# The opening blocks of a fused transformer layer: six single contraction tiles in place of two singles and two pairs

## The chip, the cores and the metric

One core of a Trainium2 chip runs the whole layer in one launch. The metric is the device time of one execution in microseconds (us). The kernel before was run three times: 2598.96, 2601.55 and 2601.9 us, median 2601.55.

## The reference

The layer has 256 latent tokens `x` and 256 context tokens `ctx`, each of width D = 2048, and condition vectors `c` and `c_ctx`. It runs a half-step feed-forward network (FFN), a token mixer (attention and a bidirectional mLSTM), and a second FFN, in float32. Only its beginning matters here:

```python
mod_l = (silu(c) @ w_mod + b_mod).reshape(B, 9, D)       # latent tokens; mod_c likewise from c_ctx
def adaln(x, g, mod, i):
    return rms_norm(x, g) * (1 + mod[:, i + 1, None, :]) + mod[:, i, None, :]
def half_step_ffn(x, mod, i, g, w_up, w_down):
    h = adaln(x, g, mod, i)
    a, b = split(h @ w_up, 2)
    return x + 0.5 * mod[:, i + 2, None, :] * ((silu(a) * b) @ w_down)
```

Before the first product `h @ w_up` can start, the shift (`mod[0]`) and the scale (`mod[1]`) are needed: two matrix products of the condition vectors with 2048 x 2048 slices of `w_mod`, 16 MB each. They belong to the channels of `h`, and the contraction of `h @ w_up` runs over just these channels.

## The kernel before

The 2048 channels are 16 contraction tiles of 128. The opening stage (lines 462 to 690) works through them in blocks, listed in `BLOCKS` (line 45): tiles 0 and 1 are blocks of their own, the other 14 go in pairs. For each block (k0, k1) the loop at line 648 does four things.

- *Modulation sums* (`mod_sums`, line 564). The weights `w_m0` come in 32 loads of 1 MB (`mod_unit`, line 557) into four buffers called `mraw`. TensorE multiplies them with the condition vectors, held as the stationary operand `cP` of 32 columns; the result goes through ScalarE (`row`), is turned by TensorE (`mod_turned`, line 588), and VectorE adds it up into `SH` (shift) and `SC` (scale). A single block takes one load for its shift and one for its scale. A pair takes four: the shift of its first tile comes in another layout and is summed by VectorE (line 660, the "still" sum, one scan for the context and one for the latent tokens, with the conditions spread over all partitions in `cB`), the shift of its second tile goes through TensorE, and so does the scale of both, in two loads with matmuls twice as wide.
- *Turning and scaling x.* TensorE turns the block's channels of the normalised tokens (`x_turned`, `to_hT`). ScalarE and VectorE apply scale and shift and split the result into a high and a low part, `hhi` and `hlo` (`x_scaled` and `affine_split`, lines 549 and 380).
- *Products* (`products`, line 407). Six result banks of 128 x 512, the first three pairs of columns of `h @ w_up`, are held in PSUM for the whole stage. Each block adds its tiles to each bank: three matmuls per tile and bank, because float32 is made of high and low parts. The weights of a block are one load (`w_pre`, 384 KB for a single block, 768 KB for a pair) that ScalarE and VectorE split (`split`, line 120) when the generator is stepped a second time. One bank's matmuls are a *unit*; a block has six.
- *Interleaving.* A block's products run while the next block's sums are made: `prods` is the previous block's generator, `following` this block's, and `steps` moves them on.

In a pair, one unit goes behind each of the three groups of modulation sums, one behind the row transposes, and two behind the transposes of x; in a single block two units go behind each of the two groups. TensorE and VectorE keep the written order throughout the stage (`Pinned`), and ScalarE does until the first pair is through (line 686). The first pair also has its products' split (`steps(following)`) and a unit behind the computation of the scale, and later blocks ahead of it. All loads of the stage are issued on SyncE's queue in the written order; the load of a block's products goes ahead of the block's last modulation load. After the stage come the long matmul phases of the first FFN.

Of the kernel before, what the change touches and what calls it, by code (L numbers as in the profile page):

```python
# [41 lines left out]

BLOCKS2 = tuple((k, k + 4) for k in range(0, 16, 4))

BLOCKS = ((0, 1), (1, 2)) + tuple((k, k + 2) for k in range(2, 16, 2))
FB = 4
CB = 512
NCB = D // CB
# [10 lines left out]
def tile_layer(ctx: ExitStack, tc: tile.TileContext, I: dict, out: bass.AP):  # L59
# [16 lines left out]
    def tbank():  # L76
        return ps["tr"].tile([P, 512], F32, tag="tr", name="tr")
# [138 lines left out]
    def scale_of(n, s, kk):  # L216

        vector[0].scalar_tensor_tensor(SC[:, n, s, kk], SC[:, n, s, kk], 1.0, gnT[:, n, kk], op0=ALU.add, op1=ALU.mult)
# [48 lines left out]
    class Beside:  # L267
# [49 lines left out]
        def steps(self):  # L317
            half = None
            while self.n < len(self.items) or self.due or self.late:
                while self.n < len(self.items):  # L320
                    h = self.items[self.n][2]
                    if h != half:
                        half = h
                        conditions({LAT: self.cB}, h, h + 1, (LAT,))
                        self.waits += WAIT
                    if self.n not in self.slots or self.done < np.interp(self.n, *zip((0, 0), *self.pace)) + self.waits:
                        break
                    self.one()
                yield
                self.done += 1  # L330
                for x in [x for x in self.due if x[0] <= self.done]:
                    self.due.remove(x)
                    self.finish(*x[1:])
                if self.late and self.late[0][0] <= self.done:
                    mod_rows_out(*self.late.pop(0)[1:])
# [71 lines left out]
    def products(n_ffn, pre, k0, k1, hhi, hlo, early=False, both=False, middle=False):  # L407

        n = (k1 - k0) * P
        most = min(2 * NPRE, 2048 // n // 2 * 2)

        def load(u0):
            nu = min(most, 2 * NPRE - u0)
            raw = raw_tile(n * nu)

            o = (2 * NPRE * k0 * P + u0 * n) * P  # L420
            tc.keep_in_program_order(nc.sync.dma_start(raw, I[f"w_pre{n_ffn}"][o : o + n * nu * P].rearrange("(p c) -> p c", p=P)))
            return raw, nu

        ahead = [load(0)]
        if early:
            wt = split(ahead[0][0], n * ahead[0][1])
        if both:
            ahead.append(load(most))
        yield
        if middle:  # L430
            wt = split(ahead[0][0], n * ahead[0][1])
            early = True
            yield
        for u0 in range(0, 2 * NPRE, most):
            raw, nu = ahead.pop(0)
            if u0 or not early:
                wt = split(raw, n * nu)
            if u0 + most < 2 * NPRE and not ahead:
                ahead.append(load(u0 + most))
            for u in range(nu):  # L440
                b = pre[(u0 + u) // 2][u % 2]
                ws = [(k, wt(slice(u * n + (k - k0) * P, u * n + (k - k0 + 1) * P))) for k in range(k0, k1)]

                for k, (wh, wl) in ws:
                    tensor[0].matmul(b, wh, hhi[:, k, :], start=k == 0, stop=False)  # L445
                    tensor[0].matmul(b, wl, hhi[:, k, :], start=False, stop=False)  # L446
                for k, (wh, wl) in ws:
                    tensor[0].matmul(b, wh, hlo[:, k, :], start=False, stop=k == KT - 1)
                yield
# [12 lines left out]
    with pool(name="st", bufs=1) as st:  # L462
# [70 lines left out]
        def others(n, act=False):  # L533
            for _ in range(n):
                x, r = rest.pop(0)
                if act:
                    scalar[0].activation(x, x, AF.Copy, scale=r)
                else:
                    vector[0].tensor_scalar(x, x, r, None, op0=ALU.mult)
# [4 lines left out]
        def x_turned(k, s, t, tb=first_tb):  # L544

            o = s * 256 + t * P
            tensor[0].transpose(tb[:, o : o + P], xs0[s, t][:, k * P : (k + 1) * P], ident)
# [9 lines left out]
        def mod_unit():  # L557
            if ready:
                return ready.pop(0)
            raw = st.tile([P, 2048], F32, tag="mraw", name="mraw", bufs=4)  # L560
            tc.keep_in_program_order(nc.sync.dma_start(raw, I["w_m0"][next(unit)]))
            return raw

        def mod_sums(i, k0, k1, last=iter(())):

            n = (k1 - k0) * P
            nk = 2048 // n
            b = tbank()[:, :n]
            for g in range(KT // nk):
                if g == KT // nk - 1:  # L570
                    steps(last)
                raw = mod_unit()
                for j in range(nk):
                    k = nk * g + j
                    q = 32 * (j % 4)
                    tensor[0].matmul(
                        b[q : q + 32, :], cP[:, k, :], raw[:, j * n : (j + 1) * n], start=k < 4, stop=k >= KT - 4, tile_position=(0, q), skip_group_check=True
                    )
                yield
            row = st.tile([P, 256], F32, tag="row", name="row", bufs=3)[:, :n]  # L580
            scalar[0].activation(row, b, AF.Copy)
            turns.append((i, k0, k1, row))

        def biased(i, k0, k1):
            dst = (SH, SC)[i][:, 0, :, k0:k1]
            vector[0].tensor_tensor(dst, dst, bmT[:, i, k0:k1].unsqueeze(1).to_broadcast([P, 2, k1 - k0]), op=ALU.add)

        def mod_turned():
            for i, k0, k1, row in turns:
                p2 = tbank()[:, : (k1 - k0) * P]  # L590
                for j in range(k1 - k0):
                    tensor[0].transpose(p2[:, j * P : (j + 1) * P], row[:, j * P : (j + 1) * P], ident)
                vector[0].tensor_reduce(
                    (SH, SC)[i][:, 0, :, k0:k1], p2.rearrange("p (k j x) -> p x k j", j=4, x=32)[:, 0:2], axis=AX.X, op=ALU.add
                )
                biased(i, k0, k1)
            turns.clear()
# [49 lines left out]
        others(2)  # L647
        for k0, k1 in BLOCKS[1:]:
            kk = slice(k0, k1)
            following = products(1, pre, k0, k1, hhi, hlo, middle=True)  # L650
            if k1 - k0 == 2:
                raw = mod_unit()
            for i in range(2):
                for _ in mod_sums(i, k0 if i else k1 - 1, k1, following if i else iter(())):
                    steps(prods, 3 - (k1 - k0))
                if rest:
                    others(2, True)
                if not i and k1 - k0 == 2:
                    for s in (CTX, LAT):
                        vector[0].scalar_tensor_tensor(  # L660
                            junk.bitcast(FP8), raw, 1.0, cB[:, s, :], op0=ALU.mult, op1=ALU.mult, accum_out=SH[:, 0, s, k0 : k0 + 1], saturate=False
                        )
                    biased(0, k0, k0 + 1)

            if k0 != 2:
                steps(following)
            mod_turned()
            if k0 != 2:
                steps(prods)
            for s in (CTX, LAT):  # L670
                scale_of(0, s, kk)
            if k0 == 2:
                steps(following)
                steps(prods)
            if k1 - k0 == 1:
                tb = tbank()
                for s in (CTX, LAT):
                    for t in range(2):
                        x_turned(k0, s, t, tb)
                x_scaled(k0, tb)  # L680
            else:
                for s in (CTX, LAT):
                    drain(to_hT([xs0[s, 0], xs0[s, 1]], 0, s, hhi, hlo, 256 * s, range(k0, k1)))
            drain(prods)
            prods = following
            if k0 == 2:
                scalar[0] = nc.scalar
            if k1 == KT:
                nc.sync.dma_start(ccd.rearrange("s (k p) -> (s k) p", p=P), cc)
# [1658 lines left out]
def _laid_out(a):  # L2348
# [27 lines left out]

    m["w_m0"] = asc(np.concatenate([u for b in BLOCKS for u in block(*b)]))
    m["w_mt"] = asc(wm[:, 2:].reshape(D, 7, KT, P).transpose(1, 2, 3, 0))
    for n in "12":
# [9 lines left out]
        loads = []  # L2389
        for k0, k1 in BLOCKS if n == "1" else BLOCKS2:  # L2390
            most = min(2 * NPRE, 2048 // ((k1 - k0) * P) // 2 * 2)
# [37 lines left out]
```

## Time and profile before

| what | us |
|---|---|
| median of three runs | 2601.55 |
| profiled execution | 2600.28 |
| its span, first to last instruction | 2598.0 |
| opening stage: end of its last product matmul | about 134.7 |
| block (2,4): sums start | 32.08 |
| block (4,6): sums start | 45.85 |
| block (6,8): sums start | 59.17 |
| block (8,10): sums start | 72.31 |

The profile is of one execution. A row of the timeline has the start, the length, the engine, the line, the operation and its operands, and in brackets how long the engine stood idle before it and what released it. A row of the stretches has the busy time of each engine between two moments, TensorE's granted clock as a share of full speed, the mean busy share of the 16 DMA engines and their rate. PE is TensorE's matmul side, DVE is VectorE, ACT is ScalarE, SP is SyncE. Where a helper records the instruction, the line in the row is the helper's (L87 is `Pinned`).

### The profile page before, as it was taken

The numbers are of one execution on the slowest core, as the hardware profiler recorded it, in microseconds if no ns is written. First come the engines' busy times: TensorE is split into PE (matmuls) and PEld (weight loads), VectorE is DVE, ScalarE is ACT, GpSimd is POOL, SyncE is SP. The second block draws the span as 40 slices with busy tenths as digits, with TensorE's granted clock in tenths as the row PEclk, the third lists the DMA queues.
The fourth block names the chain that finished last, engine by engine and source line by source line (L and its number), as shares of the span: only waits on it lengthen the run. The fifth ranks groups of instructions, "written<-read, shape, count | busy, mean of one in ns | idle before, by whom it ended". The sixth has DMA issues, their size and how long they took to land. (4 is left out here: it accounts for less than half of the span.)

```text
span 2598.0 us, 34128 instructions
## 1 busy us (share of the span) xinstructions
PE 2574.4 (99%) x12670; PEld 2145.3 (83%) x12670; DVE 2172.5 (84%) x2864; ACT 1419.1 (55%) x1822; POOL 216.1 (8%) x265
## 2 busy tenths in 40 slices
PE   8999999999999999999999999999999999999998
PEld 5788888888888888888889989888898888888887
DVE  7788888878888788888887888798889888887887
ACT  4454444544445565444454448456486676666664
POOL 0000000100000100000110000120000000000001
PEclk8999999999999999999999999999999999999999
DMA  9889999999999989989987897676768988989976
GB/s 391 346 220 265 269 286 268 263 276 285 262 287 262 281 246 242 218 216 224 229 254 261 296 321 242 235 279 215 267 239 244 276 267 259 271 275 275 260 230 174
DMA packets 127078, 680.51 MB, mean 262 GB/s; under 512 B 14136, under 2 KB 16696, under 8 KB 64832
## 3 DMA queue, kind: packets, MB, share of 16 engines
q1 hardware_dynamic: 98400, 492.73, 50.8%
q0 software_dynamic: 28512, 185.61, 36.5%
q8 instruction: 99, 1.62, 0.2%
q14 instruction: 67, 0.55, 0.1%
HBM read 660.39 MB, written 17.89 MB: 261 GB/s over the span
## 5 line engine op out<-in xcount | busy, mean ns | idle before, releaser
L128 ACT ACTIVATE hi<-raw 128x1024 fp32r<-128x1024 f32 (+2 forms) x500 | 519.0, 1042 | 424.2 <-PE mm L152 308.3
L129 DVE TENSOR_TENSOR lo<-raw,hi 128x1024 fp32r<-128x1024 f32 (+2 forms) x488 | 584.9, 1206 | 144.4 <-ACT hi L128 119.3
L128 ACT ACTIVATE hi<-chain 128x1024 fp32r<-128x1024 f32 x336 | 355.6, 1060 | 303.5 <-PE mm L152 191.4
L129 DVE TENSOR_TENSOR lo<-chain,hi 128x1024 fp32r<-128x1024 f32 x336 | 407.8, 1222 | 115.1 <-ACT hi L128 108.8
L152 PE MATMUL mm<-hi,hhi 128*128 128x512 f32 (+3 forms) x1024 | 394.0, 385 | 0.0
L152 PE MATMUL mm<-lo,hhi 128*128 128x512 f32 (+3 forms) x1024 | 387.0, 378 | 0.2 <-DVE lo L129 0.2
L152 PE MATMUL mm<-hi,hlo 128*128 128x512 f32 (+3 forms) x1024 | 386.4, 377 | 0.0
L208 DVE SCALAR_TENSOR_TENSOR junk<-sraw,cBh 128x1024 fp8e5<-128x1024 f32 x192 | 234.4, 1221 | 16.5 <-DMA sraw<-in_w_mt 14.3
L152 PEld LDWEIGHTS mm<-lo,hhi 128*128 128x128 f32 x1024 | 192.5, 188 | 34.5 <-DVE lo L129 0.6
L152 PEld LDWEIGHTS mm<-hi,hhi 128*128 128x128 f32 x1024 | 192.6, 188 | 31.0
L152 PEld LDWEIGHTS mm<-hi,hlo 128*128 128x128 f32 x1024 | 192.8, 188 | 30.7
L129 DVE TENSOR_TENSOR lo<-ra,hi 128x1024 fp32r<-128x1024 f32 x96 | 117.1, 1223 | 36.8 <-ACT hi L128 32.2
L128 ACT ACTIVATE hi<-ra 128x1024 fp32r<-128x1024 f32 x96 | 101.9, 1062 | 65.5 <-PE mm L152 49.0
L152 PE MATMUL mm<-lo,hid2h 128*128 128x512 f32 x352 | 137.1, 389 | 0.0
L152 PE MATMUL mm<-hi,hid2h 128*128 128x512 f32 x352 | 137.0, 389 | 0.0
L152 PE MATMUL mm<-hi,hid2l 128*128 128x512 f32 x352 | 136.9, 389 | 0.0
L152 PE MATMUL mm<-hi,sumshl 128*128 128x512 f32 x400 | 123.2, 389 | 0.0
L208 DVE SCALAR_TENSOR_TENSOR sr<-sr,cBl 128x1024 f32<-128x1024 f32 x84 | 102.2, 1224 | 15.1 <-DMA sr<-in_w_mt 13.6
L731 POOL DMA_DIRECT2D chain<-in_w_up1b x60 | 53.0, 884 | 729.4 <-DVE lo L129 729.4
L152 PE MATMUL mm<-hi,sumshh 128*128 128x512 f32 x352 | 108.4, 389 | 0.0
L152 PE MATMUL mm<-hhi,hi 128*128 128x512 f32 (+1 forms) x288 | 101.4, 352 | 0.0
L152 PE MATMUL mm<-hhi,lo 128*128 128x512 f32 (+1 forms) x288 | 99.0, 344 | 0.0
(490 smaller groups left out, 5457.0 us busy)
## 6 DMA issues: line engine op xcount, KB each, us to landing
raw<-in_w_dn SPq DMA_DIRECT2D x70, 1024.0 KB, 7.1
chain<-in_w_up1b POOLq DMA_DIRECT2D x60, 1024.0 KB, 10.2
sraw<-in_w_mt SPq DMA_DIRECT2D x96, 512.0 KB, 8.1
sr<-in_w_mt SPq DMA_DIRECT2D x81, 512.0 KB, 5.5
raw<-in_w_up1b SPq DMA_DIRECT2D x40, 1024.0 KB, 8.1
mraw<-in_w_m SPq DMA_DIRECT2D x32, 1024.0 KB, 8.1
raw<-in_w_up2b SPq DMA_DIRECT2D x32, 1024.0 KB, 8.1
chain<-in_w_dn POOLq DMA_DIRECT2D x30, 1024.0 KB, 8.5
```

Source lines behind the costliest of these rows:

```text
L128: scalar[0].activation(hi, src, AF.Copy)
L129: vector[0].tensor_tensor(lo, src, hi.bitcast(F32), op=ALU.subtract)
L152: tensor[0].matmul(out_ap, s, m, start=first and not n, stop=last and n == 2, skip_group_check=skip)
L208: ins = nc.vector.scalar_tensor_tensor(junk() if junk else raw, raw, 1.0, cB[s], op0=ALU.mult, op1=ALU.mult, accum_out=mT[:, i, s, kt, h : ...
L731: accum = lambda dst, src: nc.gpsimd.dma_start(dst, src, accum_op=ALU.add)
```

## The change

`BLOCKS` becomes six single blocks, tiles 0 to 5, and five pairs from tile 6 on; before it was two singles and seven pairs. The first pair, where ScalarE's written order ends and where the steps of the products stand behind the scale, is now (6,8). The weights `w_m0` and `w_pre1`, laid out on the host by the same list, change their layout with it: the still form of tiles 2 and 4 becomes the form for TensorE, and the products' weights of tiles 2 to 5 come in four loads of 384 KB in place of two of 768 KB. All bytes are as before. On each engine the instructions ahead of tile 2 and behind block (4,6) stand in the same order as before, but for the two steps that belong to the first pair.

```diff
-BLOCKS = ((0, 1), (1, 2)) + tuple((k, k + 2) for k in range(2, 16, 2))
+ALONE = 6
+BLOCKS = tuple((k, k + 1) for k in range(ALONE)) + tuple((k, k + 2) for k in range(ALONE, 16, 2))
...
-            if k0 != 2:
+            if k0 != ALONE:
                 steps(following)
             mod_turned()
-            if k0 != 2:
+            if k0 != ALONE:
                 steps(prods)
             for s in (CTX, LAT):
                 scale_of(0, s, kk)
-            if k0 == 2:
+            if k0 == ALONE:
                 steps(following)
                 steps(prods)
...
             drain(prods)
             prods = following
-            if k0 == 2:
+            if k0 == ALONE:
                 scalar[0] = nc.scalar
```

## The prediction

> **What bounds the kernel now.** I read the page first, then the stretches by block of the opening stage, then TensorE's timeline there, then the chain on ScalarE and VectorE that feeds it.
>
> ```profile
> span 2598.0 us, 34128 instructions
> PE 2574.4 (99%) x12670; PEld 2145.3 (83%) x12670; DVE 2172.5 (84%) x2864; ACT 1419.1 (55%) x1822; POOL 216.1 (8%) x265
> ```
>
> TensorE is busy for 2574.4 of 2598.0 us, so the whole span has under 24 us of idle PE. Whatever moment the opening blocks hand over to the long matmul stages, the rest of the kernel follows from it: a microsecond gained or lost before the hand-over should be a microsecond of the total. The question is thus only when PE gets through the opening blocks. By stretches (start:end, length, busy us of each engine, granted clock, DMA share, GB/s), the first three being the blocks (2,4), (4,6) and (6,8) of before, the last four windows of the clock:
>
> ```profile
> core 0: us, PE busy (x) PEld busy (x) DVE busy (x) ACT busy (x) POOL busy (x), PEclk, DMA share, GB/s
> 32.08:45.85 13.77, 11.00 (x93) 7.12 (x94) 9.11 (x17) 4.89 (x11) 0.00 (x0) 0.88 1.01 424
> 45.85:59.17 13.32, 13.32 (x112) 9.21 (x112) 10.49 (x19) 5.81 (x12) 0.00 (x0) 1.00 1.01 405
> 59.17:72.31 13.14, 13.14 (x112) 9.28 (x111) 9.69 (x18) 5.01 (x10) 0.00 (x0) 1.00 0.96 363
> 36.65:40.07 3.42, 1.39 (x18) 0.77 (x19) 2.09 (x3) 0.19 (x1) 0.00 (x0) 1.00 1.02 424
> 40.07:43.48 3.41, 3.41 (x13) 2.71 (x12) 2.05 (x8) 1.66 (x3) 0.00 (x0) 0.50 1.01 428
> 115.16:118.57 3.41, 2.38 (x24) 1.30 (x18) 3.34 (x7) 0.96 (x2) 0.00 (x0) 1.00 1.02 421
> 118.57:121.99 3.42, 3.42 (x29) 2.44 (x22) 1.74 (x8) 1.39 (x2) 0.00 (x0) 1.00 0.83 285
> ```
>
> A settled pair (59.17 to 72.31) keeps PE busy for all of its 13.14 us: it is bound by PE, VectorE has 9.69 us in it and the transfers 363 GB/s. The first pair is not: PE is busy for 11.00 of 13.77 us while the transfers run at 424 GB/s with share 1.01. There the loads are late, and one window of 3.41 us runs at a granted clock of 0.50 right after a window in which PE was busy for only 1.39 us.
>
> **The change part by part.** Tiles 2 to 5 become four blocks like block (1,2), which before already has, so its rows price them. PE's timeline (start, length, operation); "tr<-mraw" are the modulation sums, "mm" the product units of the previous block, three matmuls each, "row" and "xs" transposes:
>
> ```profile
> 27.18 1.08 PE L87 MATMUL tr<-mraw,cP 128*32 128x128 f32 x32
> 28.20 0.50 PE L87 MATMUL mm<-hhi,hi 128*128 128x512 f32 x1
> 28.54 0.40 PE L87 MATMUL mm<-hhi,lo 128*128 128x512 f32 x1
> 28.78 0.40 PE L87 MATMUL mm<-hlo,hi 128*128 128x512 f32 x1
> 29.01 0.40 PE L87 MATMUL mm<-hhi,hi 128*128 128x512 f32 x1
> 29.71 0.38 PE L87 MATMUL tr<-ident,row 128*128 128x128 f32 x2
> 29.85 0.48 PE L87 MATMUL mm<-hhi,hi 128*128 128x512 f32 x1
> 30.62 0.60 PE L87 MATMUL tr<-ident,xs 128*128 128x128 f32 x4
> 30.98 0.48 PE L87 MATMUL mm<-hhi,hi 128*128 128x512 f32 x1
> 32.08 1.08 PE L87 MATMUL tr<-mraw,cP 128*32 128x128 f32 x32 [0.16 <-DMA mraw<-in_w_m]
> 34.09 0.50 PE L87 MATMUL mm<-hlo,hi 128*128 128x512 f32 x1 [0.27 <-DVE hlo L87]
> 34.52 1.07 PE L87 MATMUL tr<-mraw,cP 128*32 128x256 f32 x16
> 35.52 0.50 PE L87 MATMUL mm<-hhi,hi 128*128 128x512 f32 x1
> 38.68 1.07 PE L87 MATMUL tr<-mraw,cP 128*32 128x256 f32 x16 [2.19 <-DMA mraw<-in_w_m]
> 42.73 1.41 PE L87 MATMUL tr<-ident,xs 128*128 128x128 f32 x8
> 45.85 1.08 PE L87 MATMUL tr<-mraw,cP 128*32 128x128 f32 x32 [0.31 <-DVE h L87]
> ```
>
> and what lies between the xs transposes at 30.62 and the matmul that needs hlo at 34.09:
>
> ```profile
> 31.26 1.02 ACT L87 ACTIVATE hhi<-tr,SH,SC 128x256 fp32r<-128x256 f32 x2 [1.79 <-PE tr L87]
> 32.17 0.56 ACT L87 ACTIVATE h<-tr,SH,SC 128x256 f32<-128x256 f32 x1
> 32.77 0.54 DVE L87 TENSOR_SCALAR h<-tr,SC,SH 128x256 f32<-128x256 f32 x1 [1.84 <-ACT h L87]
> 33.34 0.69 DVE L87 TENSOR_TENSOR hlo<-h,hhi 128x512 fp32r<-128x512 f32 x1
> ```
>
> *One single block, from its xs transposes to the next block's.* The first part is a chain: transposes, two hhi, h, h, hlo, then the matmul: 34.09 - 30.62 = 3.47 us. PE's own work beside it is the transposes 0.36 (30.62 to 30.98), the last unit 0.77 (as 29.85 to 30.62), the next block's shift sums 1.02 (27.18 to 28.20) and two matmuls 0.58 (28.20 to 28.78), together 2.73. So PE stands still for 3.47 - 2.73 = 0.74 us in every single block; the 0.27 at 34.09 is less only because PE had already waited for a load at 32.08. The second part is PE alone: the hlo matmul 0.34 (as 28.20 to 28.54), the second unit 0.70 (29.01 to 29.71), then scale sums, two units, row transposes and a unit, 3.44 (27.18 to 30.62). Period: 3.47 + 0.34 + 0.70 + 3.44 = **7.95 us**, of which 7.21 is work. A settled pair gives 6.57 per tile. More work per tile, because the sums of a pair's first shift run on VectorE (below) and its scale sums use matmuls of twice the width.
>
> *The walk.* The first xs transposes stay at 30.62: nothing ahead of them is reordered. Four periods bring the transposes of tile 5 to 30.62 + 4 x 7.95 = 62.42. Then comes block (6,8) with single products, as (2,4) is in before: chain 3.47, hlo matmul 0.43 (34.09 to 34.52), scale sums 1.00 (34.52 to 35.52), unit 0.81 (28.20 to 29.01), sums 1.00, unit 0.81, and row transposes and a unit about 1.0 (0.14 + 0.77, with one transpose more): 8.5 us, to 70.9. From its xs transposes to the sums of (8,10) before shows 3.12 us (42.73 to 45.85), 0.75 of it at half clock, and PE's work alone is 2.33 (8 transposes at 0.09 each and two units of 0.77, with little between), so I take 2.7: 73.6. Before starts that block at 72.31. **+1.3 us.** The pair that follows a block with single products took 13.32 in before, not 13.14: +0.2. Sum: **+1.5 us**; its inaccuracy is four times that of a period, say 0.2 each, plus 0.4 for the bank: about 1.2.
>
> *The same as gains and losses.* Gone: the wait of 2.19 us for a load at 38.68, and the window at half clock behind it, which cost up to 3.41 / 2 = 1.7 us, and the 0.16 at 32.08. Added: 4 x (7.21 - 6.57) = 2.6 us of PE work, and 4 x 0.74 = 3.0 us of standing still, which the pairs do not have because two units of six matmuls instead of three lie over their chain. 5.6 - 4.1 = +1.5.
>
> *Transfers.* The eight modulation loads up to tile 3 and the products' loads ahead of the last one are the same bytes in both kernels (two of 384 KB in place of one of 768 KB), so that last load still lands at about 38.6, where before waits for it; the changed kernel asks for it one chain, one matmul and one unit after tile 2's transposes: 30.62 + 7.95 + 3.47 + 0.34 + 0.70 = 43.1. The 4.5 us between are the cover; each microsecond that this load comes later than 43.1 would be paid. Afterwards a single block needs 2 x 1024 + 384 KB = 2.49 MB, 5.9 us at the 424 GB/s of the first row, under its 7.95 us. On SP's queue two loads are added; each goes ahead of a scale load and delays it by 0.9 us (384 KB at 424 GB/s): tile 2's scale load, which PE used at 32.08 in before as a shift load, lands near 32.9 and is asked for at 35.1.
>
> *VectorE and ScalarE.* Two still sums per pair go, each with a scan of 2.28 us:
>
> ```profile
> 33.95 2.28 DVE L87 SCALAR_TENSOR_TENSOR junkv<-mraw,cB 128x2048 fp8e5<-128x2048 f32 x1
> ```
>
> That is 4 x 2.3 = 9.2 us off VectorE, worth nothing in time: in a pair VectorE has 9.69 of 13.14 us and PE does not wait for it. What takes its place on VectorE and ScalarE is small operations on the chain above, already in the 3.47.
>
> **The rivals.** *A: the stall is covered.* If the chain were no longer than PE's 2.73 us, four stalls of 0.74 fall away: +1.5 - 3.0 = -1.5 us. Against it: the chain's rows add up without a gap in 30.62 to 34.09. For it: only one such block is to be seen, and there ScalarE started 0.6 us after the transposes' start.
>
> *B, slower: the clock.* A stall in every single block may bring the clock down again and again, as at 40.07. The rows bound the point from which it decides: 1.39 us busy in a window was followed by 0.50, 2.38 us by 1.00. With a stall of 0.74 a window has 3.41 - 0.74 = 2.67 us busy, above the upper row, which speaks against it; but should the transposes (0.36) and the sums, which use 32 of 128 columns (1.02), weigh little, 1.3 us are left, and the two rows no longer decide. Price: 1.7 us for each half-clock window, less the stall that then vanishes inside it, so 1.0 to 1.7, in five blocks 5 to 8.5; I take 6.5: +8 in all. [...]
>
> *C: something faster that no row shows*, such as a wait of the long stages that goes with the new phase. PE's idle after the opening stage is too small for 5 us in any one place, so this is unlikely.
>
> **How the numbers follow.** The profiled execution took 2600.28 us, 1.27 under the median of 2601.55. Sum against its own time: 2601.8; against the median: 2603.0, which is the forecast. Chances: forecast 0.61 (2601.8 to 2604.2), A 0.16 (2600.0), B 0.16 (2609.5), C 0.07 (under 2596.3). The range reaches from A, less 1.5 for the spread of runs (2598.96 to 2601.9), to B: 2598.5 to 2609.5. About 0.2% (5.2 us) is what a measurement of this kernel can tell from no change: forecast and A lie within it, B is beyond it, C on the other side. Faster 0.07, same 0.77, slower 0.16.
>
> **What would show it.** In the changed kernel's PE timeline: no wait for mraw between 32 and 60 us; sums of single blocks about 7.95 us apart, each with a hlo wait of 0.6 to 0.75; the first sums of (8,10) near 73.6; settled pairs at 13.14 after that; granted clock 1.00 from 26.4 on. Wrong: a period under 7.4 us (A), a 0.50 window between 30 and 70 us (B), a wait for mraw in a single block (the transfers), or a shift at the hand-over that the end of the span does not repeat.

## The result and the profile after

The changed kernel takes 2604.19 us (median of 21 runs, 2600.58 to 2607.39); before takes 2600.42 us (21 runs, 2597.96 to 2603.9). The ratio is 1.0014, with a 95% interval of 1.0008 to 1.002: slower by 3.6 us, between 2.1 and 5.2. The forecast was +1.5 us: the direction came true, the size is more than double. The prediction held that only 0.2% (5.2 us) could be told from no change; with 21 runs of each, 3.6 us can.

The page of the changed kernel, to be held against the page of before, shows 4.9 us more span and 4.7 us more PE:

```profile
span 2602.9 us, 34420 instructions
PE 2579.1 (99%) x12800; PEld 2148.1 (83%) x12800; DVE 2164.8 (83%) x2870; ACT 1420.7 (55%) x1830; POOL 215.7 (8%) x265
```

Its PE timeline in the opening stage: xs transposes (each marks one block), two of the waits, and the first matmul behind the stage. Lines are one higher than in before.

```profile
31.54 0.60 PE L88 MATMUL tr<-ident,xs 128*128 128x128 f32 x4
39.60 0.60 PE L88 MATMUL tr<-ident,xs 128*128 128x128 f32 x4
43.07 0.51 PE L88 MATMUL mm<-hlo,hi 128*128 128x512 f32 x1 [0.50 <-DVE hlo L88]
...
63.69 0.60 PE L88 MATMUL tr<-ident,xs 128*128 128x128 f32 x4
72.32 1.03 PE L88 MATMUL tr<-ident,xs 128*128 128x128 f32 x8
75.96 1.08 PE L88 MATMUL tr<-mraw,cP 128*32 128x128 f32 x32 [1.23 <-DMA mraw<-in_w_m]
82.64 1.07 PE L88 MATMUL tr<-mraw,cP 128*32 128x256 f32 x16 [1.42 <-DMA mraw<-in_w_m]
86.85 1.04 PE L88 MATMUL tr<-ident,xs 128*128 128x128 f32 x8
...
139.86 0.39 PE L153 MATMUL mm<-hhi,hi 128*128 128x512 f32 x1
```

Four periods lie between 31.54 and 63.69, 8.04 us each, every one with a wait of 0.5 for hlo. Then come two waits for loads that I had not forecast. In before the last row's place is 134.70. PE's waits in the stage, grouped (total, times, longest), first before, then after:

```profile
PE tr L87 <- DMA mraw<-in_w_m: 3.4, 3, 2.2
PE tr L87 <- DVE h L87: 0.3, 1, 0.3
PE mm L87 <- DVE hlo L87: 0.3, 1, 0.3
...
PE tr L88 <- DMA mraw<-in_w_m: 3.9, 3, 1.4
PE mm L88 <- DVE hlo L88: 2.5, 5, 0.5
```

I call *stage* the time from the first xs transposes (30.62 in before, 31.54 after; what lies ahead of them is the same in both) to the first matmul behind it: 104.08 us before, 108.32 after, +4.24. By pieces, from xs transposes to xs transposes:

| piece | before | after | difference | forecast |
|---|---|---|---|---|
| tiles 2 to 5 as singles, against two settled pairs | 26.28 | 32.15 | +5.87 | +5.52 |
| first pair, with single products | 12.11 | 8.63 | -3.48 | -3.6 |
| the pair behind it | 12.72 | 14.53 | +1.81 | -0.4 |
| the remaining pairs (two of before's stand in the first row) and the end | 79.25 - 26.28 | 53.01 | +0.04 | 0 |

The last row holds a wait for a load in the last pair in both kernels, 1.03 us before (at 118.24) and 1.29 after (at 123.41).

That the first transposes came 0.92 us later is a difference of these two executions, not of the kernels: nothing ahead of them is changed, and the second profiles below have 30.77 and 31.04. The end of the span shows the shift of the hand-over again: 5.16 us at 139.86, 4.9 at the end.

Since single executions of either kernel spread over 6 us, the variants below are judged by the stage in their profiles first, by the ratio of runs second. A second profile of each kernel gives the stage's own spread:

> The kernel before once more, for a second profile: stage 104.1 within 0.5, the wait of about 2.2 us for mraw at 38 to 39 us and a half-clock window behind it again.

Stage 102.78 us, with the 2.21 us wait again and a window at half clock (39.3 to 42.7 us) right behind it:

```profile
38.84 1.51 PE L87 MATMUL tr<-mraw,cP 128*32 128x256 f32 x16 [2.21 <-DMA mraw<-in_w_m]
```

Most of the 1.3 us less is the wait of 1.03 us at 118.24 in the first profile, which this one does not have.

> The changed kernel once more, for a second profile: stage 108.3 within 0.5, five waits of 0.5 for hlo, two of 1.2 to 1.4 for mraw in block (8,10), no window at half clock from 30 us to the end of the stage. If the waits for mraw were chance, they are absent.

Stage 106.37. PE's waits in it:

```profile
PE mm L88 <- DVE hlo L88: 2.7, 6, 0.5
PE tr L88 <- DMA mraw<-in_w_m: 1.5, 2, 0.8
```

The five waits for hlo are there again (the sixth, 0.17, is in the last pair, at 130.02). The waits for mraw are two in place of three, and shorter: 0.72 in block (8,10) at 80.66, where the first profile has 1.42, and 0.80 in the last pair at 120.96, where it has 1.29. The first sums of (8,10), which waited 1.23 for a load, now wait 0.33 for the bank. So the stalls are fixed, and the late loads vary by some 2.4 us between executions. Difference of the second profiles: 106.37 - 102.78 = 3.6 us.

### The profile page after: what moved, and what is told of

The parts are those of the page before. It is cut to its first block, busy times and chain, and to the rows that moved or that the text cites. A ratio compares the mean times of both kernels' runs of the same rounds, so it can differ in the third digit from the quotient of the medians.

```text
span 2602.9 us, 34420 instructions
## 1 busy us (share of the span) xinstructions
PE 2579.1 (99%) x12800; PEld 2148.1 (83%) x12800; DVE 2164.8 (83%) x2870; ACT 1420.7 (55%) x1830; POOL 215.7 (8%) x265
```

## The experiments

**One unit over the chain.** Tests whether the stalls cost.

```diff
                 for _ in mod_sums(i, k0 if i else k1 - 1, k1, following if i else iter(())):
-                    steps(prods, 3 - (k1 - k0))
+                    steps(prods, 1 if i else 3 - (k1 - k0))
...
-            if k0 != ALONE:
+            single = k1 - k0 == 1
+            if k0 != ALONE and not single:
                 steps(following)
...
+            if single:
+                steps(following)
             if k0 == ALONE:
```

> In single blocks one unit of products moves from behind the scale sums to behind the xs transposes, and the split of the block's own weights goes behind the computation of the scale. Theory (a stall of about 0.5 to 0.7 us at the hlo matmul of every single block is part of the loss): the five waits for hlo go to 0.1 or less, the period of a single block falls from 8.04 to about 7.3 us, the hand-over to settled pairs comes about 3 us earlier, and the whole is about 0.8 us over before (2601) instead of 3.8. Rival (the stalls are not what costs; the loss comes from the loads or from the later stages): period under 8 us, but the first pair waits as much longer for its loads, whole unchanged at +3.8.

PE's timeline of this run, two singles and the waits behind them:

```profile
37.47 0.60 PE L88 MATMUL tr<-ident,xs 128*128 128x128 f32 x4
44.79 0.60 PE L88 MATMUL tr<-ident,xs 128*128 128x128 f32 x4
...
72.34 1.08 PE L88 MATMUL tr<-mraw,cP 128*32 128x128 f32 x32 [1.39 <-DMA mraw<-in_w_m]
79.00 1.07 PE L88 MATMUL tr<-mraw,cP 128*32 128x256 f32 x16 [1.40 <-DMA mraw<-in_w_m]
```

No wait for hlo is left in a single block, and the period is 7.32 us. The chain itself is as long as before: hlo ends 3.42 us behind the start of the transposes (40.89 against 37.47), in the changed kernel 3.41 (43.01 against 39.60). So it is the unit over the chain that takes the stall away, and not the later split. The stalls are a real part of the loss in the stage: 0.72 us per single block, 2.9 in four.

The stage is 104.79, 3.5 less than the changed kernel's first profile and 1.6 less than its second. Not all of the 3.5 is the edit's: 1.3 of it is the wait in the last pair, which this profile lacks, as does before's second. The waits for loads behind the singles stay, one of 0.43 joins them, and the first pair and the one behind it take 0.7 us more than in the first profile. Ratio to before 1.0006 (0.9997 to 1.0015): the runs alone do not tell the theory's +0.8 us from the rival's +3.8.

**A fifth buffer for one load.** Tests whether the late loads come from buffers that come free late.

```diff
-            raw = st.tile([P, 2048], F32, tag="mraw", name="mraw", bufs=4)
-            tc.keep_in_program_order(nc.sync.dma_start(raw, I["w_m0"][next(unit)]))
+            n = next(unit)
+            raw = raw_tile() if n == 16 else st.tile([P, 2048], F32, tag="mraw", name="mraw", bufs=4)
+            tc.keep_in_program_order(nc.sync.dma_start(raw, I["w_m0"][n]))
```

> The first load of block (8,10) takes a free buffer of another pool, so that the four mraw buffers no longer hold it back; all else as in the changed kernel. Theory (the two waits of 1.23 and 1.42 us for mraw in block (8,10) come from buffers that come free late, not from the channel): both fall under 0.3, a wait of about 0.4 for the bank shows instead, hand-over about 2.2 us earlier, whole about +1.6 over before. Rival (the channel is full there): the loads land when they did, both waits stay, whole +3.8.

The first sums of block (8,10), and the xs transposes in it:

```profile
74.35 1.08 PE L88 MATMUL tr<-mraw,cP 128*32 128x128 f32 x32 [0.32 <-DVE h L88]
83.94 1.03 PE L88 MATMUL tr<-ident,xs 128*128 128x128 f32 x8
```

Both waits for mraw are gone and the bank shows instead. From xs transposes (71.61) to xs transposes (83.94) the block takes 12.33 us, 2.2 less than in the first profile after. Stage 104.99, 3.3 less than that profile (1.4 less than the second); the rest of the 3.3 is nearly all the wait in the last pair, which is absent here too. The whole does not show it: ratio 1.001 (1.0001 to 1.0019); the profiled execution spans 2607.3 us, 9.3 more than before's, most of it lost later in the kernel. In this profile the buffers account for the waits. But with nothing changed the second profile after waited only 0.72 us in this block, so one profile does not exclude chance (the last two runs with six singles return to it), and the price in the whole stays open.

**Four singles; fourteen singles.** `ALONE = 4` and `ALONE = 14`.

> Four single blocks, the pairs from tile 4 on. Theory (each single costs 1.47 us more than half a pair, and the first pair waits about 2.2 us for its successor's loads wherever it stands): 2 x 1.47 = 2.9 us less than with six, +0.9 over before, with two waits for mraw of over a microsecond in block (6,8). Rival (the loss is proportional to the number of tiles made single, 3.8 / 4 each): +1.9, and no waits.

PE's waits for loads in it, now in block (6,8):

```profile
58.51 1.08 PE L88 MATMUL tr<-mraw,cP 128*32 128x128 f32 x32 [0.42 <-DMA mraw<-in_w_m]
65.18 1.07 PE L88 MATMUL tr<-mraw,cP 128*32 128x256 f32 x16 [1.36 <-DMA mraw<-in_w_m]
```

Stage 103.29, within the two values of before; ratio 1.0002 (0.9993 to 1.001). Against the changed kernel's two profiles that is 5.0 and 3.1 less; 2.9 were expected. The interval holds the theory's +0.9 us and the rival's +1.9 alike. The waits, which the rival did not have, moved with the first pair, though only one of them is over a microsecond.

> Fourteen single blocks and one pair. Theory: eight singles more at 1.47 each, without the 2.2 us of waits as no pair follows the first: 3.8 + 11.8 - 2.2 = +13.4 over before; granted clock 1.00 throughout the singles although each has a stall. Rival (proportional): +11.4. Rival (the clock falls in some of the many stalls): windows at 0.50, over +17.

Stretches of this run (thirteen singles; the last pair; two windows of the clock), and PE's waits for hlo:

```profile
31.55:136.49 104.94, 98.45 (x1144) 68.87 (x1142) 42.21 (x134) 37.70 (x91) 0.00 (x0) 1.00 0.85 328
136.49:152.20 15.71, 12.57 (x51) 9.65 (x50) 14.33 (x19) 6.99 (x12) 0.00 (x0) 0.89 0.75 270
140.90:144.30 3.40, 1.05 (x5) 0.88 (x6) 3.35 (x4) 0.43 (x1) 0.00 (x0) 1.00 0.79 260
144.30:147.70 3.40, 3.40 (x10) 2.63 (x9) 2.73 (x4) 0.60 (x1) 0.00 (x0) 0.50 0.93 388
```

```profile
PE mm L88 <- DVE hlo L88: 9.0, 14, 2.5
```

2617.77 us, ratio 1.007 (1.0057 to 1.0082), +15.9 by the medians (13.4 expected); stage 120.71, +16.6 over before. With thirteen stalls of 0.5 us in a row the granted clock was 1.00 from 31.55 to 136.49 us, so the clock as a rival falls for the singles. The 3 us too much are at the end, as the trace reads (no run tests it): with the first pair last, the next stage's split stands on VectorE between this pair's h and hlo (1.23 us at 141.37), PE waits 0.63 us for hhi and 2.52 for hlo, and only then does a window at 0.50 follow.

**Both edits.** 

> Both edits at once, six singles: one unit moved over the chain, and the first load of block (8,10) in a buffer of another pool. From the first xs transposes to the first matmul behind the stage, before has 104.1 us, the changed kernel 108.3. Theory (two separate losses, each gone with its edit, 3.5 and 3.3): 101.5, so 2.6 less than before, and the whole 2.6 under before. Rival (they share a cause: with shorter singles the loads are late again): waits for mraw over 1 us in block (8,10), stage 104.5.

The rival came true: stage 104.96, as with either edit alone (104.79 and 104.99). Its waits, and the stretches up to them, in which the last two columns are the DMA share and GB/s:

```profile
PE tr L88 <- DMA mraw<-in_w_m: 2.8, 2, 1.6
```

```profile
45.00:52.00 7.00, 7.00 (x88) 5.08 (x87) 2.69 (x8) 2.83 (x8) 0.00 (x0) 1.00 0.95 348
52.00:58.00 6.00, 6.00 (x83) 4.31 (x81) 2.86 (x10) 1.81 (x5) 0.00 (x0) 1.00 0.77 268
76.00:82.00 6.00, 4.40 (x36) 2.66 (x29) 3.84 (x5) 1.96 (x3) 0.00 (x0) 1.00 1.02 428
```

My theory of two separate losses falls. While the later singles run the channel is not used up (348 and 268 GB/s), because all four buffers are full: from 45 to 58 us the load queue waits 10.7 of 13 us for TensorE's sums, which free a buffer.

```profile
SPq L563 <- PE tr L88: 10.7, 3, 4.3
```

Behind the singles the channel is used up (428 GB/s at a share of 1.02), and PE waits. Shorter singles (7.32 us each against 8.04) leave it less time. If so, one more load held ahead must help (the edit is against the run with both):

```diff
-            raw = raw_tile() if n == 16 else st.tile([P, 2048], F32, tag="mraw", name="mraw", bufs=4)
+            raw = raw_tile() if n in (12, 16) else st.tile([P, 2048], F32, tag="mraw", name="mraw", bufs=4)
```

> Six singles, the unit moved over the chain, and the first loads of blocks (6,8) and (8,10) both in buffers of another pool, so that one load more stands ahead while the singles run. Theory (while the singles run the channel idles because all four buffers are full, 268 to 348 GB/s, and the two pairs behind them then need more than it gives): 2.4 us of transfer come earlier, the waits of 0.31, 1.15 and 1.60 us of the run with one such load shrink to about 0.6 together, stage 102.5 instead of 105.0. Rival (the channel is full and the buffers do not matter): waits and stage as with one, 105.

The same views of this run:

```profile
45.00:52.00 7.00, 7.00 (x88) 5.11 (x87) 2.73 (x9) 2.86 (x7) 0.00 (x0) 1.00 1.02 421
52.00:58.00 6.00, 6.00 (x83) 4.29 (x82) 2.63 (x8) 1.75 (x4) 0.00 (x0) 1.00 1.00 420
76.00:82.00 6.00, 5.96 (x44) 4.31 (x43) 4.13 (x11) 1.13 (x3) 0.00 (x0) 1.00 1.00 423
```

```profile
PE tr L88 <- DVE h L88: 0.3, 1, 0.3
```

The channel now runs at 421 and 420 GB/s during the same singles (and at 308 in the next 6 us, where it had 418), the load queue's waits for TensorE's sums fall from 10.7 to 5.1 us, no wait for mraw is left, the bank's 0.34 is the only one, and the stage is 102.02 us. That is 2.9 less than with one load, and a little more than the 2.4 by which late loads vary between executions, so the reading rests on the channel and the load queue as much as on the stage. Ratio 0.9998 (0.999 to 1.0007). The changed kernel's interval, 1.0008 to 1.002, lies wholly above this one, each against before's own runs beside it: with the stalls and the late loads both removed, the loss is gone from the whole too.

**Four singles with the edits.** First with the unit over the chain alone, then with one and with two loads in the other pool (`n == 12`; `n in (8, 12)`).

> Four singles with the unit moved over the chain, buffers as they were. Theory: stage 103.3 - 2.2 = 101.1 with one wait for mraw of 1.4 in block (6,8), whole 3.0 under before.

> Four singles, with both edits (the load of another pool is the first of block (6,8)). Theory: stage 103.3 of four singles alone, less 3 x 0.72 for the stalls and 1.4 for the wait: 99.8, whole about 4.3 under before. Rival (with fewer singles the channel itself is what the first pair waits for): a wait for mraw stays, stage about 101.

> The same with four singles (first loads of blocks (4,6) and (6,8)). Theory: there the channel is full until about 45 us and idles only briefly, so a second buffer brings less: waits of 0.23, 0.31 and 1.34 fall to about 1 together, stage 101 instead of 102.1; whole 2 to 3 under before.

Without the pool: stage 103.31, not 101.1; three waits for mraw of 0.42, 1.28 and 1.46 us take back what the stalls gave, and the theory fails. Ratio 1.0005 (0.9996 to 1.0015). With one load: stage 102.13, waits of 0.23 and 1.34 for mraw and 0.31 for the bank, nearer to the rival's 101 than to the theory's 99.8; ratio 1.0 (0.9991 to 1.0009). With two: stage 101.47, waits of 0.57 and 0.35 for mraw and 0.32 for the bank, about as expected; 2598.61 us, ratio 0.9992 (0.9983 to 1.0001). This is the version with the lowest median, and its interval still holds 1: a gain of 2 us is likely, not shown.

**What before loses.** 

```diff
+            n = next(unit)
+            if n == 7:
+                return held[0]
             raw = st.tile([P, 2048], F32, tag="mraw", name="mraw", bufs=4)
...
+            held[:] = [raw]
             return raw
```

> The kernel before with the eighth modulation load left out (its matmuls read the seventh load's tile again, so the scale sums of tiles 2 and 3 are not the reference's). It prices what the singles gain. Theory (before loses a wait of 2.19 us and a half-clock window behind it to this load): the wait and the window at half clock go, from the first xs transposes to those of block (2,4) 8.6 us instead of 12.1, stage about 100.6. Rival (only the wait counts, the clock window has another cause): 9.9 us, a window at 0.50 remains.

From the first xs transposes to those of block (2,4):

```profile
30.38:39.32 8.94, 8.22 (x87) 5.02 (x86) 6.92 (x15) 3.39 (x7) 0.00 (x0) 1.00 1.00 419
```

8.94 us instead of 12.11, granted clock 1.00 throughout: the wait and the half-clock window belong together. Two shorter waits for loads, 0.48 and 0.24 us, are in the 8.94. The stage is 99.78 (4.3 less than the first profile of before, 3.0 less than the second), the ratio 0.9989 (0.998 to 0.9998). Leaving a load out also spares the channel 1 MB, so stage and ratio are more than the price of this one wait.

## Why the prediction was right, and where its size was off

- *A single block costs more than half a pair.* Right. Forecast 7.95 us, measured 8.04; the stall forecast as 0.74 was worth 0.72 when it was taken away (8.04 - 7.32), and shows as 0.50 in the rows mainly because the matmul ahead of it is drawn 0.40 us long, to a modelled end, where matmuls that wait for nothing start 0.24 apart (28.54 and 28.78 in before). The missing 0.09 is the longer step from a unit to the sums that follow it (0.32 us, 43.88 to 44.20, where the forecast had 0.23, 29.48 to 29.71 in before); over four blocks 0.35 us.
- *The wait for the eighth load and the half-clock window go.* Right: the first pair took 8.63 us (8.62 in the second profile) after the singles where 8.5 were forecast, and no window at half clock lies between 30 us and the end of the stage in either profile. Leaving the load out of before confirmed the price from the other side (8.94).
- *The two waits for the first pair's successor.* This is the step that missed the size, in the part on transfers: "Afterwards a single block needs 2 x 1024 + 384 KB = 2.49 MB, 5.9 us at the 424 GB/s of the first row, under its 7.95 us." True of the singles, but I did not ask it of the first pair. In its 8.6 us PE passes only single products, while the block behind it needs a pair's loads, 4.98 MB or 11.7 us at 424 GB/s. Nor did I ask who holds loads ahead: four buffers, full while the later singles run (the channel moved 253 and 281 GB/s from 50 to 62 us). I had the third row of the table at -0.4 (the half-clock time in before's 3.12 us). It was +1.8 in the first profiles and +0.8 in the second (13.11 against 12.34); in the run with the fifth buffer, where no load is late, it is -0.4 as forecast (12.33 against 12.72). That is 2.2 of the 2.7 us by which the stage's sum was short in the first profiles, and 1.2 of 2.1 in the second. Another 0.8 there is the wait in the last pair, which one profile of before has as well (1.03), so that nothing shows it to be the change's.
- *The hand-over carries to the end.* Right in these two profiles: 5.16 us there, 4.9 at the end of the span; in the second profiles 3.86 and 4.0. Most of the runs' spread of 6 us is made later: the profile with the fifth buffer hands over at 135.85, 1.15 us behind before's, and ends 9.3 us later. Such a spread hides a gain of 2 us in the stage from eleven runs.
- *The time itself.* The forecast stretch of 2601.8 to 2604.2 us holds 2604.19, but that is luck: it stood on before's median of three runs, 2601.55, and 21 runs put before at 2600.42. With before at 2601.55, 3.6 us more would have been 2605.2.
- *Rival A* (the stall is covered) fell with the waits for hlo in both profiles; an edit to the order makes it true. *Rival B* (the clock) fell: the granted clock was 1.00 in all singles of both profiles (31.54 to 63.69 and 31.04 to 63.16 us), also with thirteen in a row. No run shows its 6.5 us for half-clock windows in five blocks; a stall of 0.5 us in 8 us left the clock at full. *Rival C*: nothing of it was seen.

The changed kernel's windows around its 1.42 us wait are another bound for the clock. In before's trace the granted clock is 0.50 from 16.17 to 26.41 us (10.24), from 40.07 to 43.48 (3.41) and again from 2593.24: three, four, one and 747 times 3.413 us lie from one change to the next. The two rows are laid on this spacing from the changed kernel's own change at 2598.6 us:

```profile
79.56:82.98 3.42, 2.00 (x18) 1.30 (x18) 3.38 (x5) 1.58 (x2) 0.00 (x0) 1.00 1.01 429
82.98:86.39 3.41, 3.41 (x30) 2.43 (x22) 1.41 (x7) 0.38 (x1) 0.00 (x0) 1.00 1.01 428
```

2.00 us busy in 3.42 was followed by full clock, 1.39 (before) and 1.05 (fourteen singles) by half. The profile's busy time does not decide it alone, so the prediction's two rows (1.39 and 2.38 us) bound no single point. In before a window with 2.91 us busy, at full clock, was followed by half:

```profile
12.76:16.17 3.41, 2.91 (x19) 1.67 (x10) 3.20 (x16) 2.95 (x9) 0.78 (x1) 1.00 1.01 428
16.17:19.59 3.42, 2.18 (x5) 1.33 (x5) 3.11 (x13) 2.71 (x9) 1.10 (x3) 0.50 1.00 419
```

What else counts stays open.

## What to carry to other kernels

Smaller blocks ask for their loads in smaller steps, which here took the wait for the eighth load (2.19 us) away, but leave less of the previous block's work to lie over the chain from transposes to operands (a stall worth 0.72 us a block here); count that chain against what is queued behind it, and move a unit over it before changing the block size. Where block sizes change, compare the loads of the next block with the work of this one at the seam, not only inside each regime, and ask which buffers let loads run ahead: a channel that idles in one stretch and is full in the next, as here (268 and then 428 GB/s in the run with both edits), may be short of buffers and not of bandwidth.

## What the runs showed of the hardware that was not expected

The clock is less touchy than rival B supposed: thirteen stalls of 0.5 us in a row left it at 1.00, and a window with 2.00 of 3.42 us busy kept it. Nor is it a plain matter of PE's busy time, as before's window with 2.91 us busy and half clock behind it shows. The late loads depend on the execution: the same kernel waited 3.9 us for mraw in one profile of its stage and 1.5 in another.
